# Wide modulation sets on VectorE, and products with a column of ones at their end

## The chip, the cores and the metric

The kernel runs on one core of a Trainium2 chip, as one program with one launch. The metric is the device time of an execution in microseconds (us), from the median of several runs. The engines are named as in the profile: PE is TensorE's products and PEld its weight loads, DVE is VectorE, ACT is ScalarE, POOL is GpSimd, SP is SyncE, whose queue issues the transfers.

## What is computed

One layer of an encoder block on 256 tokens of width 2048, in float32, with adaLN modulation from one conditioning vector `c`:

```python
c_act = jax.nn.silu(c)
mod = (c_act @ ada_w[l] + ada_b[l])[:, None, :]
shift_a, scale_a, gate_a, shift_f, scale_f, gate_f = jnp.split(mod, N_MOD, axis=-1)

h = rmsnorm(x, norm1_w[l]) * (1.0 + scale_a) + shift_a
proj = h @ w_in[l]
...
mixed = jnp.concatenate([ret_out, mla_out], axis=-1) @ w_o[l]
x = x + gate_a * mixed

h = rmsnorm(x, norm2_w[l]) * (1.0 + scale_f) + shift_f
ff = (jax.nn.silu(h @ w_gate[l]) * (h @ w_up[l])) @ w_down[l]
x = x + gate_f * ff
```

`ret_out` comes from eight retention heads with rotary positions and decay, `mla_out` from eight attention heads with compressed latents. `ada_w` is 2048 by 12288, so the one vector `c_act` meets 100 MB of weights, a third of all that the kernel reads. Each of the six sections (shift, scale and gate for the mixer, the same for the feed-forward) has 2048 columns.

## The kernel before, in words

All weights are streamed from memory in the order of use. A projection's weights come in tiles of 512 KB (tile `stg`, six buffers). `split_weights` (L119) issues the transfer on SP, lets ScalarE round the tile to a high part (`whi`, L124) and VectorE subtract it for a low part (`wlo`, L126), three buffers each. TensorE multiplies in three passes, high by high, high by low, low by high (L132 to L134), with 512 columns moving. `run` (L152) walks a list of steps; up to three tiles are loaded and split ahead of the step that uses them (`LOOK`).

The modulation is made by `ada_set` (L174). A set is `nk` times 128 columns of one section. Its weights come in the same 512 KB tiles, one **unit** each. A string of 0 and 1 says for each set which engine takes it:

- on TensorE (L196), the vector in a padded 32-column tile `c_pad` is the stationary operand and 256 columns move; the bank is copied to `ada_acc` by ScalarE at the end (L206);
- on VectorE, each row block of the unit is multiplied by the vector's value of its partition and added to the accumulator `ada_acc` (L198 the first time, L200 after), at the width of the set, 512 columns at most.

The 128 partitions of the accumulator have to be summed at a set's end. `finish` (L202) adds the bias row of a gate section (L211, L212). `spread` (L214) handles the two kinds of sections: for a gate it multiplies the accumulator by a matrix of ones (L218), which lays the sum on all partitions; for shift and scale it transposes each 128 columns (L222) so that VectorE can reduce them to a column (L226), then adds the bias (L227) and, for a scale section, makes the gain (L230).

The two sections that the input projection needs are made beside its column groups. The mixer's own list is `plan` (L742 to L786): the input projection's last chunks, latent and attention steps (`mla_step`), retention heads (`ret_scores`, `ret_out`) with tiles of the output projection as filler, and the rest of that projection. The sections GT_A (the mixer's gate) and SC_F, SH_F (scale and shift of the feed-forward, their first 1536 columns) are cut into ten sets, `early`; their 80 units are put between the plan's steps (L791 to L805) by two counters, one of TensorE time, one of transfer time, at a rate `ADA_RATE`. `ADA_PE2` gives sets 1, 6 and 7 of them to TensorE. VectorE's order in time is made by a scheduler from this list, so small VectorE work such as the rotary tables (L296 to L306, 32 operations on 128x96) can stand elsewhere than in the code.

## Time and profile before

| | us |
|---|---|
| median of three runs | 1261.68 |
| the three runs | 1259.57, 1261.85, 1261.68 |
| the profiled execution's own time | 1259.87 |
| its span, first to last instruction | 1257.9 |
| PE busy | 1217.3 (97%) |
| PEld busy | 973.0 (77%) |
| DVE busy | 841.1 (67%) |
| ACT busy | 600.9 (48%) |
| mean granted clock of TensorE | .994 |

The durations in this document come from that one profiled execution; its time is 1.8 us under the median. A busy time is the union of an engine's instructions, so overlapping instructions count once. An instruction's own duration is longer than its distance to the next one where the two overlap; for a price the distance from start to start is read. A float32 product of TensorE leaves two records and two weight loads in the trace, a transposition one of each.

### The profile page before, as it was taken

To read this page: it belongs to the slowest core of one execution; us is meant where nothing else is said; L and a number is where in the kernel's file an instruction comes from. 1 tells how busy PE (TensorE), PEld (TensorE's weight loads), DVE (VectorE), ACT (ScalarE), POOL (GpSimd) and SP (SyncE) were. 2 spreads that over 40 slices of the span, in tenths; PEclk is the share of its full clock that TensorE was granted. 3 is DMA by queue.
4 is the path that set the end of the run, shared out by engine and by line. 5 is a ranking of instruction groups with operands and counts; after the bars stand their busy time and mean duration, and the time that the engine had idled before them with its cause. 6 is when DMAs were issued, how large, how long until landed. Compare 5 with 4: busy or idle time off the path is not lost.

```text
span 1257.9 us, 16210 instructions
## 1 busy us (share of the span) xinstructions
PE 1217.3 (97%) x6022; PEld 973.0 (77%) x6022; DVE 841.1 (67%) x1157; ACT 600.9 (48%) x812; POOL 2.2 (0%) x10
## 2 busy tenths in 40 slices
PE   5899999999999999899999999999999999999997
PEld 2676667789886787678888888888888888888885
DVE  2596988889997997885555556656655454554544
ACT  4553454545557554745444444444444443444433
POOL 0000000000000000000000000000000000000000
PEclk9999999999999999899999999999999999999999
DMA  8989898888878987897676658766775655555562
GB/s 330 324 302 310 296 326 295 291 311 298 323 243 297 319 289 268 323 356 222 218 226 225 202 170 284 235 198 212 262 224 189 218 188 197 194 191 194 191 200 85
DMA packets 88800, 315.28 MB, mean 251 GB/s; under 512 B 10249, under 2 KB 10377, under 8 KB 88209
## 3 DMA queue, kind: packets, MB, share of 16 engines
q1 hardware_dynamic: 88720, 314.24, 73.4%
q8 instruction: 47, 0.77, 0.2%
q14 instruction: 33, 0.26, 0.1%
HBM read 312.11 MB, written 2.10 MB: 250 GB/s over the span
## 4 chain that ended last, share of the span: by engine, by line
PE 85%; DVE 7%; DMA 4%; ACT 2%; issue 2%; SPq 0%; ACTq 0%; DVEq 0%
PE bank L133 25%; PE bank L134 25%; PE bank L132 25%; DMA stg<-in_stream 4%; DVE wlo L126 3%; PE bank L196 3%; PE bank L148 2%; DVE ada_acc L200 2%; ACT whi L124 1%; PE bank L625 1%; PE bank L614 1%; PE bank L513 0%; PE bank L537 0%; PE bank L512 0%; PE bank L222 0%
## 5 line engine op out<-in xcount | busy, mean ns | idle before, releaser
L126 DVE TENSOR_TENSOR wlo<-stg,whi 128x1024 fp32r<-128x1024 f32 (+2 forms) x400 | 478.8, 1199 | 331.8 <-ACT whi L124 330.3
L124 ACT CAST whi<-stg 128x1024 fp32r<-128x1024 f32 (+2 forms) x400 | 413.2, 1034 | 526.1 <-PE bank L134 411.9
L132 PE MATMUL bank<-whi,actt 128*128 128x512 f32 (+1 forms) x1184 | 457.7, 392 | 11.4 <-ACT whi L124 8.2
L133 PE MATMUL bank<-wlo,actt 128*128 128x512 f32 (+1 forms) x1184 | 460.7, 389 | 6.9 <-DVE wlo L126 6.2
L134 PE MATMUL bank<-whi,actt 128*128 128x512 f32 (+1 forms) x1184 | 458.1, 387 | 0.2 <-DVE actt L145 0.2
L132 PEld LDWEIGHTS bank<-whi,actt 128*128 128x128 f32 x1184 | 221.8, 189 | 63.6 <-ACT whi L124 12.0
L133 PEld LDWEIGHTS bank<-wlo,actt 128*128 128x128 f32 x1184 | 223.2, 189 | 61.5 <-DVE wlo L126 16.7
L134 PEld LDWEIGHTS bank<-whi,actt 128*128 128x128 f32 x1184 | 223.1, 188 | 44.8 <-DVE actt L145 0.9
L200 DVE SCALAR_TENSOR_TENSOR ada_acc<-stg,c_act,ada_acc 128x512 f32<-128x512 f32 (+1 forms) x240 | 175.3, 731 | 21.2 <-DMA stg<-in_stream 18.3
L132 PE MATMUL bank<-whi,ap 128*128 128x512 f32 x352 | 137.0, 389 | 0.0
L134 PE MATMUL bank<-whi,ap 128*128 128x512 f32 x352 | 136.9, 389 | 0.0
L133 PE MATMUL bank<-wlo,ap 128*128 128x512 f32 x352 | 136.9, 389 | 0.0
L132 PEld LDWEIGHTS bank<-whi,ap 128*128 128x128 f32 x352 | 66.1, 188 | 13.8
L133 PEld LDWEIGHTS bank<-wlo,ap 128*128 128x128 f32 x352 | 66.1, 188 | 13.7
L134 PEld LDWEIGHTS bank<-whi,ap 128*128 128x128 f32 x352 | 66.1, 188 | 13.6
L196 PE MATMUL bank<-stg,c_pad 128*32 128x256 f32 x544 | 48.6, 418 | 11.4 <-DMA stg<-in_stream 11.3
L196 PEld LDWEIGHTS bank<-stg,c_pad 128*32 128x32 f32 x544 | 13.0, 112 | 35.5 <-issue 26.7
L851 ACT ACTIVATE sgs<-bank 128x512 f32<-128x512 f32 x22 | 13.1, 597 | 10.5 <-PE bank L134 9.8
L145 DVE TENSOR_TENSOR actt<-hfull,actt 128x256 fp32r<-128x256 f32 x40 | 16.3, 419 | 2.4 <-ACT actt L144 2.3
L853 DVE TENSOR_TENSOR sgs<-bank,sgs 128x512 f32<-128x512 f32 x22 | 14.3, 683 | 0.6 <-PE bank L134 0.6
L833 DVE TENSOR_TENSOR ap<-bank,ap 128x512 fp32r<-128x512 f32 x22 | 14.1, 682 | 0.0
L226 DVE TENSOR_REDUCE mod<-bank 128x4 f32<-128x512 f32 (+3 forms) x18 | 8.0, 444 | 8.9 <-PE bank L222 8.7
(219 smaller groups left out, 708.2 us busy)
## 6 DMA issues: line engine op xcount, KB each, us to landing
stg<-in_stream SPq DMA_DIRECT2D x568, 512.0 KB, 4.4
stg<-in_stream SPq DMA_DIRECT2D x16, 288.0 KB, 3.5
stg<-in_stream SPq DMA_DIRECT2D x8, 384.0 KB
xt<-in_x SPq DMA_DIRECT2D x2, 1024.0 KB
acc_cq<-in_x SPq DMA_DIRECT2D x8, 256.0 KB, 4.7
out<-x SPq DMA_DIRECT2D x8, 256.0 KB, 2.9
acc_k<-in_rows SPq DMA_DIRECT2D x1, 1024.0 KB, 7.5
fw<-in_rows SPq DMA_DIRECT2D x1, 1024.0 KB
```

What stands on the lines that cost most here:

```text
L124: S.copy(hi, stg)
L126: V.tensor_tensor(lo, stg, hi.bitcast(F32), op=ALU.subtract)
L132: PE.matmul(o, lhsT=ah, rhs=whi, start=first, stop=False)
L133: PE.matmul(o, lhsT=ah, rhs=wlo, start=False, stop=False)
L134: PE.matmul(o, lhsT=al, rhs=whi, start=False, stop=last)
L145: V.tensor_tensor(dst[:, k, T:2 * T], tmp, dst[:, k, 0:T].bitcast(F32), op=ALU.subtract)
L148: PE.transpose(b[:, j, tb * P:(tb + 1) * P], src, ident)
L196: PE.matmul(a[q:q + 32, c:c + wide], lhsT=c_pad[:, k], rhs=w[:, j], start=c == 0 and k < 4, stop=c + wide == n and k >= KT - 4)
L200: V.scalar_tensor_tensor(out=a, in0=w[:, j], scalar=c_act[:, k:k + 1], in1=a, op0=ALU.mult, op1=ALU.add)
L833: V.tensor_tensor(ap[:, ks, T:2 * T], b, ap[:, ks, 0:T].bitcast(F32), op=ALU.subtract)
L851: S.activation(sg, o[tb], AF.Silu)
L853: V.tensor_tensor(sg, o[tb], sg, op=ALU.mult)
```

## The change

Five things change in `ada_set` and around it.

1. Sets that VectorE makes may be 1024 columns wide. GT_A becomes two sets of eight blocks (before, four of four), SC_F and SH_F a set of eight and one of four each. A unit then holds one row block of 1024 columns and takes one operation in place of two.
2. The end of a shift or scale set is a product of each 128x128 block, as the stationary operand, with one column of ones. Its result is the wanted column, so the reduction is gone and one addition from the bank remains.
3. A gate set on VectorE begins with a clear by GpSimd and a transfer of the bias row into row 0 of the accumulator, and its first step accumulates too. The addition at the end is gone.
4. `ADA_PE2` leaves one set, the narrow one of SC_F, on TensorE; two sets' worth of units goes to VectorE.
5. The 80 units are spread evenly: after each step of the plan as many units as its share of the plan's cost (2.7 for a tile, 1 for any other step), so that they are through at 95% of it.

The angle tiles of the rotary tables take buffers of the decay tiles' tag, and the tile `dg` those of `hfull`.

```diff
--- before.py
+++ after.py
@@ -40,9 +40,8 @@
 GROUPS = [(0, 2), (2, 4), (6, 4), (10, 6)]
 ADA_PE = "10010100101101"
 LEAD = [1, 1, 3, 3, 3, 3, 3]
-ADA_PE2 = "010000110000"
-ADA_RATE = 0.8
-ADA_AHEAD = 0
+ADA_PE2 = "000100"
+ADA_END = 0.95
 LOOK = 3
 FILL_A = [2, 2]
 FILL_M = [3, 0, 1, 0, 4, 2, 1, 3, 2, 2]
@@ -178,7 +177,8 @@
         acc = {}
 
         def acc_tile():
-            return (pool or late["pool"]).tile([P, n], F32, name="ada_acc", tag="ada_acc", bufs=2 if pool else 1, padded_shape=[P, 512])
+            most = 1024 if pool else 512
+            return (pool or late["pool"]).tile([P, n], F32, name="ada_acc", tag="ada_acc", bufs=2 if pool else 1, padded_shape=[P, most])
 
         def load(c, t):
             w = wp.tile([P, kk, wide], F32, name="stg", tag="stg", bufs=6)
@@ -188,16 +188,23 @@
         def body(c, t, w):
             if c == 0 and t == 0:
                 acc["t"] = bank() if on_pe else acc_tile()
+                if not on_pe and rowdst is not None:
+                    G.memset(acc["t"], 0.0)
+                    bias_row(acc["t"])
             a = acc["t"]
             for j in range(kk):
                 k = t * kk + j
                 if on_pe:
                     q = 32 * (k % 4)
                     PE.matmul(a[q:q + 32, c:c + wide], lhsT=c_pad[:, k], rhs=w[:, j], start=c == 0 and k < 4, stop=c + wide == n and k >= KT - 4)
-                elif k == 0:
+                elif k == 0 and rowdst is None:
                     V.tensor_scalar(out=a, in0=w[:, j], scalar1=c_act[:, 0:1], scalar2=None, op0=ALU.mult)
                 else:
                     V.scalar_tensor_tensor(out=a, in0=w[:, j], scalar=c_act[:, k:k + 1], in1=a, op0=ALU.mult, op1=ALU.add)
+
+        def bias_row(a):
+            r0 = (R_GA if sec == GT_A else R_GF) + k0 * P
+            SY.dma_start(a[0:1, :], rows[:, r0:r0 + n])
 
         def finish():
             a = acc["t"]
@@ -205,26 +212,25 @@
                 b, a = a, acc_tile()
                 S.copy(a, b[:, 0:n])
             acc["a"] = a
-            if rowdst is not None:
-                r0 = (R_GA if sec == GT_A else R_GF) + k0 * P
+            if on_pe and rowdst is not None:
                 br = wp.tile([1, n], F32, name="bias_row", tag="stg", bufs=6)
-                SY.dma_start(br, rows[:, r0:r0 + n])
+                bias_row(br)
                 V.tensor_tensor(a[0:1, :], a[0:1, :], br, op=ALU.add)
 
         def spread():
             a = acc["a"]
+            if rowdst is not None:
+                for c in range(0, n, CH):
+                    b = bank()
+                    PE.matmul(b, lhsT=ones, rhs=a[:, c:c + CH], start=True, stop=True)
+                    S.copy(rowdst()[:, k0 * P + c:k0 * P + c + CH], b)
+                return
             b = bank()
-            if rowdst is not None:
-                PE.matmul(b[:, 0:n], lhsT=ones, rhs=a, start=True, stop=True)
-                S.copy(rowdst()[:, k0 * P:k0 * P + n], b[:, 0:n])
-                return
             for j in range(nk):
-                PE.transpose(b[:, j * P:(j + 1) * P], a[:, j * P:(j + 1) * P], ident)
+                PE.matmul(b[:, j:j + 1], lhsT=a[:, j * P:(j + 1) * P], rhs=ones[:, 0:1], start=True, stop=True)
             ks = slice(sec * KT + k0, sec * KT + k0 + nk)
             m = mod[:, ks]
-            parts = b[:, 0:n].rearrange("p (j q) -> p j q", q=P)
-            V.tensor_reduce(out=m, in_=parts[:, :, ::32] if on_pe else parts, axis=AX.X, op=ALU.add)
-            V.tensor_tensor(m, m, col[:, C_ADAB + ks.start:C_ADAB + ks.stop], op=ALU.add)
+            V.tensor_tensor(m, b[:, 0:nk], col[:, C_ADAB + ks.start:C_ADAB + ks.stop], op=ALU.add)
             if sec in (SC_A, SC_F):
                 g, nw = (gain_a, C_N1) if sec == SC_A else (gain_f, C_N2)
                 V.scalar_tensor_tensor(out=g[:, k0:k0 + nk], in0=m, scalar=1.0, in1=col[:, nw + k0:nw + k0 + nk], op0=ALU.add, op1=ALU.mult)
@@ -291,8 +297,8 @@
         SY.dma_start(freq, rows[:, R_FREQ:R_FREQ + 96].partition_broadcast(P))
         V.tensor_copy(posf, post)
         for tb in range(NB):
-            a = mid.tile([P, 96], F32, name="ang", tag="ang", bufs=2)
-            n = mid.tile([P, 96], F32, name="turns", tag="turns", bufs=2)
+            an = mid.tile([P, 2, 96], F32, name="ang", tag="dec", bufs=2)
+            a, n = an[:, 0], an[:, 1]
             V.tensor_scalar(out=a, in0=freq, scalar1=posf[:, tb:tb + 1], scalar2=None, op0=ALU.mult)
             for magic in (1.5 * 2.0 ** 34, 1.5 * 2.0 ** 23):
                 V.tensor_scalar(out=n, in0=a, scalar1=1.0 / TWO_PI, scalar2=magic, op0=ALU.mult, op1=ALU.add)
@@ -722,7 +728,7 @@
         rsqrt(stat[:, 30:32], stat[:, 28:30], 1.0 / D)
         b = bank()
         for tb in range(NB):
-            dg = mid.tile([P, P], F32, name="dg", tag="dg", bufs=2)
+            dg = mid.tile([P, P], F32, name="dg", tag="hfull", bufs=2)
             V.tensor_scalar(out=dg, in0=ident, scalar1=stat[:, 30 + tb:31 + tb], scalar2=None, op0=ALU.mult)
             PE.matmul(b[:, tb * P:(tb + 1) * P], lhsT=ones, rhs=dg, start=True, stop=True)
         S.copy(rstd_b, b[:, 0:T])
@@ -785,23 +791,19 @@
             plan.append(f(turn_x2, n - 1))
         plan += c[2:]
 
-    early = [(GT_A, 4 * i, 4, lambda: gate_a) for i in range(4)]
-    early += [(sec, k, min(4, K_LATE - k), None) for sec in (SC_F, SH_F) for k in range(0, K_LATE, 4)]
+    early = [(GT_A, 8 * i, 8, lambda: gate_a) for i in range(2)]
+    early += [(sec, k, min(8, K_LATE - k), None) for sec in (SC_F, SH_F) for k in range(0, K_LATE, 8)]
     units = ada_stream(mid, [(*st, on == "1") for st, on in zip(early, ADA_PE2)])
-    pe = dma = 0.0
-    for s in plan:
+    cost = [2.7 if s[0] == "w" else 1.0 for s in plan]
+    done, used = 0.0, 0
+    for s, c in zip(plan, cost):
         steps.append(s)
-        if s[0] == "w":
-            pe += 2.6
-            dma += 1.5
-        else:
-            pe += 1.0
-        for _ in range(2):
-            if units and dma < pe * ADA_RATE + ADA_AHEAD:
-                steps += units.pop(0)
-                pe += 0.5
-                dma += 1.5
-    for u in units:
+        done += c
+        want = min(len(units), int(len(units) * done / (ADA_END * sum(cost))))
+        for u in units[used:want]:
+            steps += u
+        used = want
+    for u in units[used:]:
         steps += u
 
     def gate_f_tile():
```

Where the order of the instructions moves, it does so as follows. First VectorE, where the last column group of the input projection begins. `dec` is a decay tile of the retention, `ang`, `turns` and `sc_t` belong to the rotary tables, `wlo` to the weight split. Before, in the middle of the second column group, a little earlier than this place:

```order
L609 TENSOR_SCALAR dec<-dist,lg 128x384
L302 TENSOR_SCALAR sc_t<-ang 128x96
L610 SCALAR_TENSOR_TENSOR dec<-dist,lg,dec 128x384
L350 TENSOR_TENSOR acc_k<-acc_k,bank 128x512 x2
L126 TENSOR_TENSOR wlo<-stg,whi 128x1024
L303 TENSOR_SCALAR ang<-ang 128x96
L609 TENSOR_SCALAR dec<-dist,lg 128x384
L304 TENSOR_SCALAR turns<-ang 128x96
L610 SCALAR_TENSOR_TENSOR dec<-dist,lg,dec 128x384
L305 TENSOR_TENSOR ang<-ang,turns 128x96
L306 TENSOR_SCALAR sc_t<-ang 128x96
L126 TENSOR_TENSOR wlo<-stg,whi 128x1024
```

Now, right before the first accumulate of the first gate set:

```order
L305 TENSOR_SCALAR ang<-ang 128x96 x2
L307 SCALAR_TENSOR_TENSOR ang<-ang 128x96 x6
L308 TENSOR_SCALAR sc_t<-ang 128x96 x2
L309 TENSOR_SCALAR ang<-ang 128x96 x2
L310 TENSOR_SCALAR ang<-ang 128x96 x2
L311 TENSOR_TENSOR ang<-ang 128x96 x2
L312 TENSOR_SCALAR sc_t<-ang 128x96 x2
L125 TENSOR_TENSOR wlo<-stg,whi 128x576
L203 SCALAR_TENSOR_TENSOR ada_acc<-stg,c_act,ada_acc 128x1024
L356 TENSOR_TENSOR acc_cq<-acc_cq,bank 128x512 x2
```

The rotary operations have left the projection's middle and stand in one block ahead of the first 1024-column accumulate; the decay tiles stand later, in the attention steps.

Second, TensorE at the start of the retention steps. Before:

```order
L614 MATMUL bank<-qT,kT 128x256 x2
L148 MATMUL bank<-ident,rout 128x128 x8
L196 MATMUL bank<-stg,c_pad 32x256 x8
L614 MATMUL bank<-qT,kT 128x256 x2
L625 MATMUL bank<-acc_v,rP 128x128 x4
L196 MATMUL bank<-stg,c_pad 32x256 x4
L222 MATMUL bank<-ident,ada_acc 128x128 x4
L148 MATMUL bank<-ident,att 128x128 x8
```

Now:

```order
L620 MATMUL bank<-qT,kT 128x256 x2
L199 MATMUL bank<-stg,c_pad 32x256 x4
L147 MATMUL bank<-ident,rout 128x128 x8
L620 MATMUL bank<-qT,kT 128x256 x2
L631 MATMUL bank<-acc_v,rP 128x128 x4
L199 MATMUL bank<-stg,c_pad 32x256 x4
L230 MATMUL bank<-ones,ada_acc 128x1 x8
L147 MATMUL bank<-ident,att 128x128 x8
```

Modulation products (L196, now L199) are eight instead of twelve in these rows, and the four transpositions with the identity are products with the column of ones (L230), in two passes each.

Third, VectorE in the second half of the output projection, up to the first update of `x`. Before:

```order
L126 TENSOR_TENSOR wlo<-stg,whi 128x1024 x2
L200 SCALAR_TENSOR_TENSOR ada_acc<-stg,c_act,ada_acc 128x512 x2
L126 TENSOR_TENSOR wlo<-stg,whi 128x1024
L200 SCALAR_TENSOR_TENSOR ada_acc<-stg,c_act,ada_acc 128x512 x3
L126 TENSOR_TENSOR wlo<-stg,whi 128x1024
L684 TENSOR_TENSOR x_0_3928<-x_0_3928,bank 128x512
L684 TENSOR_TENSOR x_1_3936<-x_1_3936,bank 128x512
L685 TENSOR_TENSOR x_0_3928<-x_0_3928,gate_a 128x512
```

Now:

```order
L125 TENSOR_TENSOR wlo<-stg,whi 128x1024
L203 SCALAR_TENSOR_TENSOR ada_acc<-stg,c_act,ada_acc 128x1024
L125 TENSOR_TENSOR wlo<-stg,whi 128x1024
L201 TENSOR_SCALAR ada_acc<-stg,c_act 128x512
L203 SCALAR_TENSOR_TENSOR ada_acc<-stg,c_act,ada_acc 128x512 x2
L125 TENSOR_TENSOR wlo<-stg,whi 128x1024
L203 SCALAR_TENSOR_TENSOR ada_acc<-stg,c_act,ada_acc 128x512 x2
L690 TENSOR_TENSOR x_0_3793<-x_0_3793,bank 128x512
L125 TENSOR_TENSOR wlo<-stg,whi 128x1024
L691 TENSOR_TENSOR x_0_3793<-x_0_3793,gate_a 128x512
```

Where the last narrow accumulates stood, there is now a 1024-column one, and a narrow set (SH_F's second) only begins here (L201), so that it goes on behind the first update of `x`.

## Rows read from the trace of the kernel before

**Rows 1.** Windows by stage, all engines: length, busy us (instructions), granted clock, DMA share, GB/s.
```profile
24.00:192.00 168.00, 157.52 (x858) 113.29 (x858) 130.02 (x219) 82.55 (x115) 0.00 (x0) 0.99 0.88 307
192.00:261.00 69.00, 67.59 (x415) 52.27 (x413) 54.27 (x97) 36.61 (x63) 0.00 (x0) 1.00 0.86 298
261.00:376.00 115.00, 114.10 (x632) 97.72 (x633) 107.75 (x176) 63.44 (x119) 0.00 (x0) 1.00 0.85 294
376.00:434.00 58.00, 58.00 (x389) 42.22 (x389) 49.12 (x114) 37.34 (x65) 0.00 (x0) 1.00 0.84 305
434.00:490.00 56.00, 56.00 (x269) 46.74 (x268) 52.73 (x76) 32.94 (x50) 0.00 (x0) 1.00 0.88 300
490.00:503.00 13.00, 13.00 (x87) 9.34 (x87) 7.83 (x12) 4.83 (x11) 0.00 (x0) 1.00 0.57 187
```

**Rows 2.** The same windows, line L196 (modulation products on TensorE) alone.
```profile
192.00:261.00 69.00, 7.62 (x80) 1.83 (x80) 1.00 0.86 298
...
376.00:434.00 58.00, 10.02 (x128) 2.62 (x128) 1.00 0.84 305
```

**Rows 3.** The same windows, line L200 (modulation accumulates on VectorE) alone.
```profile
192.00:261.00 69.00, 11.21 (x15) 1.00 0.86 298
...
376.00:434.00 58.00, 8.92 (x12) 1.00 0.84 305
434.00:490.00 56.00, 13.45 (x19) 1.00 0.88 300
```

**Rows 4.** Window from 288 to 320 us, all engines (columns as in rows 1).
```profile
288.00:320.00 32.00, 31.41 (x210) 28.26 (x209) 30.65 (x51) 18.87 (x34) 0.00 (x0) 1.00 0.92 321
```

**Rows 5.** Timeline of TensorE around one modulation unit: start us, us, operation.
```profile
100.85 0.39 PE L134 MATMUL bank<-whi,actt 128*128 128x512 f32 x1
101.17 0.64 PE L196 MATMUL bank<-stg,c_pad 128*32 128x256 f32 x8
101.74 0.50 PE L132 MATMUL bank<-whi,actt 128*128 128x512 f32 x1
```

**Rows 6.** Timeline of VectorE in attention.
```profile
320.94 0.68 DVE L515 TENSOR_REDUCE st<-bank 128x2 f32<-128x512 f32 x1
321.54 0.74 DVE L200 SCALAR_TENSOR_TENSOR ada_acc<-stg,c_act,ada_acc 128x512 f32<-128x512 f32 x1
322.20 0.16 DVE L516 TENSOR_SCALAR st<-st 128x2 f32<-128x2 f32 x1
```

**Rows 7.** VectorE groups by shape: busy us, mean ns, idle before; last three: 140 to 172 us.
```profile
L200 DVE SCALAR_TENSOR_TENSOR ada_acc<-stg,c_act,ada_acc 128x512 f32<-128x512 f32 x225 | 168.0, 748 | 21.0 <-DMA stg<-in_stream 18.3
...
L200 DVE SCALAR_TENSOR_TENSOR ada_acc<-stg,c_act,ada_acc 128x256 f32<-128x256 f32 x15 | 7.2, 482 | 0.2
...
L301 DVE SCALAR_TENSOR_TENSOR ang<-turns,ang 128x96 f32<-128x96 f32 x12 | 2.7, 252 | 0.0
...
L610 DVE SCALAR_TENSOR_TENSOR dec<-dist,lg,dec 128x384 f32<-128x384 f32 x2 | 1.2, 618 | 0.0
L609 DVE TENSOR_SCALAR dec<-dist,lg 128x384 f32<-128x384 f32 x2 | 0.8, 415 | 0.0
```

**Rows 8.** Timeline of TensorE in the retention steps.
```profile
427.38 0.60 PE L222 MATMUL bank<-ident,ada_acc 128*128 128x128 f32 x4
427.82 1.06 PE L625 MATMUL bank<-acc_v,rP 128*128 128x128 f32 x8
428.71 1.03 PE L614 MATMUL bank<-qT,kT 128*128 128x256 f32 x4
```

**Rows 9.** Weight loads of TensorE by line: count, busy us, mean ns.
```profile
L625 PEld LDWEIGHTS bank<-acc_v,rP 128*128 128x128 f32 x64 | 8.0, 191 | 1.8 <-issue 1.6
...
L222 PEld LDWEIGHTS bank<-ident,ada_acc 128*128 128x128 f32 x64 | 7.6, 142 | 5.4 <-ACT ada_acc L206 2.2 <-issue 1.6 <-ACT dec L611 0.4
```

**Rows 10.** GpSimd groups by line and shape.
```profile
L259 POOL MEMSET c_pad<- 128x512 f32 x1 | 0.5, 525 | 0.0
```

**Rows 11.** DMA issues of the page: tile, count, KB each, median us from issue to landing.
```profile
stg<-in_stream SPq DMA_DIRECT2D x568, 512.0 KB, 4.4
```

## The prediction

> **What bounds the kernel now.** I read four views, from coarse to fine. The windows by stage come first [rows 1]. I cut the span where the work changes: input projection with the first two modulation sections (24 to 192 us), its last column group (192 to 261), attention and the second retention half (261 to 376), the retention steps (376 to 434), the output projection (434 to 503), and feed-forward. The reader is to compare, in each row, TensorE's busy time with the length: 157.52 of 168, then 67.59 of 69, 114.10 of 115, and 58.00 of 58, 56.00 of 56, 13.00 of 13. TensorE is the bound from 192 us on, at a granted clock of .99 to 1.00; it has 10.5 us of idle time before 192, and nearly none behind. VectorE is second: 107.75 of 115 (.937) in one stretch, 52.73 of 56 (.942) in another. So an edit pays only where it takes work off TensorE, and it costs where it lifts VectorE to the length of the stretch.
>
> The windows by line come second: who does the modulation units (one unit is 512 KB of modulation weights), in which stretch [rows 2, 3]. On TensorE a unit leaves 8 records: 80 records are 10 units in 192 to 261, and 128 are 16 in 376 to 434. On VectorE a unit is two 512-column operations: 15 accumulates plus the set's first multiply there are 8 units, and 19 plus one in 434 to 490 are 10.
>
> Third come timelines for prices (next part). Fourth comes the highest VectorE share that I found over 32 us ahead of the feed-forward: 30.65 of 32, which is .958, with TensorE at 31.41 [rows 4].
>
> **The change, part by part: the prices.**
>
> - A unit on TensorE. Between two neighbouring products of the projection the step is .23 us; across a unit's 8 records it is .89 (100.85 to 101.74) [rows 5]. So a unit costs .66 us of TensorE.
> - A 512-column accumulate on VectorE: .66 us from its start to the next (321.54 to 322.20); a reduction .60 (320.94 to 321.54) [rows 6].
> - A 1024-column accumulate: no row has one. The forms of 256 and 512 columns take 482 and 748 ns, 266 for each 256 columns more [rows 7]. So 512 columns more add .53 to the .66: 1.19 us. The upper bound is two narrow ones, 1.32. I take 1.19: it is the straight continuation of two rows of the same operation. A unit on VectorE thus falls from 1.32 to 1.19.
> - A transposition of the end of a set: four take .44 (427.38 to 427.82), .11 each. What replaces it is a product of the 128x128 accumulator, as stationary operand, with one column. No row has one. The nearest is the retention's fp32 product, same stationary shape, 128 columns moving: four in .89 (427.82 to 428.71), .22 each [rows 8]. It issues two weight loads of 191 ns where the transposition issues one of 142 [rows 9], and those loads do not shrink with the moving columns. Below, a product could cost what a transposition does, .11; above, both loads one after another, .38. I take .22, +.11 against the transposition: the row with the same loads.
>
> The Trainium skill ("TensorE: Matmul & The Clock Gate", Back-to-back issue gap) gives matmuls of 1 to 64 columns an issue floor of about 25 ns. Two passes would make an estimated .05 per product, and the sum would be 11 us lower over 64 products. The rows speak against it, since the two loads are there whatever the columns.
>
> - Gate sets on VectorE: the accumulator is cleared by GpSimd and the bias row lands in it by DMA before the first accumulate, in place of an add behind the last one. A 128x512 clear takes 525 ns, so some 1.0 for 1024 columns, and a transfer lands in 4.4 us [rows 10, 11]: 5.4 in all. In the order, the tile is asked for while 22 VectorE rows stand ahead of the first accumulate, so I cost it at nothing; without that cover it is up to 5.4 us once. SP waits for the clear, and the weight loads behind it on that queue wait too, but three tiles are ahead. Lower bound: 0.
>
> **The same by stretch.** The order shows where things now stand. The rotary tables (32 small VectorE operations) leave 147 to 168 us and stand as one block just ahead of the first wide accumulate. Four more units reach the output projection, seven fewer the retention steps.
>
> - 24 to 192. TensorE gets 24 products more dear by .11: +2.6. VectorE loses the rotary block, two decay tiles and three reductions. The block's 32 operations of 128x96 last up to 252 ns [rows 7]; an accumulate overlaps the next one by .09 (748 long, .66 apart), so I put them .14 apart, 4.4 us in all. A decay tile's two operations, 415 and 618 ns, come by the same overlap to .85, two tiles to 1.7, three reductions to 1.8: together 7.9 of 130.02. TensorE's 10.5 us of idle time covers most of the 2.6. I take -.3, between -3 (the idle time shrinks with VectorE's load) and +3.
> - 192 to 261. TensorE loses 8 of its 10 units, 5.3 us, and pays .4 for four products: 62.7. VectorE: 54.27 - 10.6 (16 narrow operations) + 20.2 (17 wide) + 4.4 (rotary) = 68.3 of 69. Here VectorE becomes the longer engine. At a share of 1 the stretch shrinks by .7; at the best share seen, .958, it takes 71.3, +2.3. Middle: **+1.0**, bounds -4.9 (TensorE alone decides) and +2.3.
> - 261 to 376. Four transpositions leave (-.4). VectorE gains the two decay tiles (+1.7) and loses 27 x 1.32 - 28 x 1.19 = 2.3, a reduction and the bias adds, so it is eased a little, and I let half of TensorE's .9 idle go: -.8, bounds -1.3 and 0.
> - 376 to 434. TensorE: 58.0 - 8 units (5.3) + 12 products (1.3) = 54.0. VectorE: 49.1 - 12 narrow accumulates (7.9) - 1.4 for their first multiply and the reductions + 10 x 1.19 = 51.7, which at .958 also gives 54.0. **-4.0**, bounds -4.3 and -2.5.
> - 434 to 503. TensorE: 12 products for 8 transpositions, +1.8. VectorE in 434 to 490: 52.7 - 12.5 (19 narrow) - 1.7 + 7 x 1.19 + 8 x 1.32 = 57.4 of 56, at .958 59.9, +3.9. The 13 us behind have VectorE at 7.83, but TensorE full, so lost time is not recovered. Middle: **+2.5**, bounds 1.8 and 3.9.
> - Feed-forward: 8 products (+.9) against two reductions: +.1, bounds -.5 and +.9.
>
> Sum: -.3 + 1.0 - .8 - 4.0 + 2.5 + .1 = **-1.5 us**. It is made against the profiled execution's 1259.87, which lies 1.8 below the median of the three runs; I set it against the median, 1261.68: **1260.2**. A measurement of this kernel can tell about .2%, 2.5 us, from no change.
>
> **The rivals.**
>
> *B, TensorE stays the bound.* VectorE runs at a share near 1 where it must, or work slides into neighbouring slack; then 192 to 261 shrinks by 4.9 and the output projection pays 1.8: -.3 - 4.9 - .8 - 4.0 + 1.8 + .1 = -8.1, 1253.6. For it: in 434 to 490 TensorE was at 56.00 of 56 with VectorE at .942, so that share costs nothing yet. Against it: 68.3 of 69 leaves no room for any wait.
>
> *C, slower: VectorE sets the pace where its share would pass what it has held.* The weight split of each tile queues behind wide accumulates that wait for their transfer, and TensorE waits for the split. Price: the share VectorE held over 115 us, .937, holds as a ceiling. Then 192 to 261 takes 68.3 / .937 = 72.9 (+3.9), 376 to 434 takes 55.2 (-2.8), 434 to 490 takes 61.3 (+5.3): -.3 + 3.9 - .8 - 2.8 + 5.3 + .1 = +5.4, 1267.1. It decides from a needed share of .94 on. Against it: .958 occurs without loss over 32 us.
>
> *D, slower by the gate bias.* The first wide accumulate waits the 5.4 us out, and the splits stand behind it: -1.5 + 5.4 = +3.9, 1265.6. The 22 rows ahead speak against it.
>
> *E, slower by the new ends.* The two loads of a one-column product run one after another, since so short a product hides nothing: .38 in place of .22, 64 x .16 = 10.2 more, 1270.4. The .22 spacing at two 191 ns loads speaks against it, but there a 128-column product ran meanwhile.
>
> A rule of the Trainium skill stands on E's side: "TensorE: Matmul & The Clock Gate", Terms, calls the transpose mode 4 times faster for FP32, so the change gives up a cheap form; by it a product would cost an estimated .44, 64 x .22 = 14.1 us over my price and 1274.3. The two rows of .11 and .22 show a factor of two for the same shapes, not four.
>
> That the change doesn't do what it says I rule out by the order: 64 transpositions became 64 products, and one modulation set of the mixer stays on TensorE.
>
> **How the numbers follow.** The forecast's chance is .50, of which .34 within .2% (it lies 1.0 us inside that bound) and .16 faster. B gets .22, faster. C gets .18, D .04, E .06, all slower. So faster .38, same .34, slower .28. The range reaches from just under B to C, 1253.0 to 1267.0; outside are the lower part of B (.07), the upper part of C (.05) and E (.06).
>
> **What would show it.** 128 fewer TensorE records of modulation products; wide accumulates some 1.27 long and 1.19 apart; one-column pairs .22 apart. VectorE's share at .95 or more in the last column group and the output projection, with weight loads there waiting for the split's low part. The retention steps are shorter by about 4. It is wrong if the last column group is shorter by 4 or more (B), if the output projection is longer by over 4 (C), if VectorE stands idle over 2 us ahead of the first wide accumulate of a gate (D), or if one-column products stand over .3 apart (E).

## The result, and the profile after

The changed kernel takes 1273.99 us (median of four runs, 1273.2 to 1275.23) against 1261.32 of the kernel before: a ratio of 1.011, 95% interval 1.0095 to 1.0125. It is slower by 12.7 us between the medians and by 12 to 16 by the interval, where 1.5 less was forecast, and lies above the range. The profiled execution has a span of 1272.2 us against 1257.9.

The windows of the changed kernel, all engines, cut at the same projection products of TensorE as [rows 1] (columns as there; PE and DVE busy are the first and third figures):

```profile
25.90:200.40 174.50, 163.04 (x882) 117.94 (x882) 121.43 (x176) 76.89 (x107) 0.00 (x0) 0.99 0.85 293
200.40:277.10 76.70, 68.93 (x360) 54.47 (x358) 65.15 (x127) 40.66 (x68) 1.91 (x2) 0.96 0.80 281
277.10:389.40 112.30, 111.95 (x625) 96.40 (x623) 103.30 (x143) 64.63 (x121) 0.00 (x0) 1.00 0.84 294
389.40:442.90 53.50, 53.50 (x336) 42.86 (x336) 47.49 (x105) 36.35 (x63) 0.00 (x0) 1.00 0.80 284
442.90:505.20 62.30, 60.04 (x285) 49.59 (x285) 58.77 (x77) 33.23 (x50) 0.00 (x0) 0.97 0.87 299
505.20:518.40 13.20, 13.20 (x89) 9.65 (x87) 7.29 (x13) 4.95 (x12) 0.00 (x0) 1.00 0.65 236
...
590.00:1272.00 682.00, 672.81 (x3008) 556.76 (x3006) 371.24 (x365) 286.68 (x311) 1.05 (x2) 1.00 0.61 205
```

The feed-forward is the same 682 us. The retention steps (389 to 443) really are shorter, 53.5 us for 58; the first part (174.5 for 168), the last column group (200 to 277, 76.7 for 69) and the output projection (443 to 505, 62.3 for 56) are longer. The delay builds up and falls back, read at the start of the same low-part subtraction on VectorE in both traces (400 of them, counted from 0):

| subtraction | 0 | 36 | 48 | 54 | 66 | 72 | 102 | 114 | 138 | 399 |
|---|---|---|---|---|---|---|---|---|---|---|
| before, us | 21.9 | 139.7 | 184.4 | 203.7 | 238.0 | 254.7 | 367.8 | 432.2 | 515.6 | 1241.6 |
| after, later by | 2.5 | 4.6 | 8.0 | 9.6 | 15.6 | 17.4 | 11.0 | 4.2 | 15.4 | 14.1 |

So 8 us are lost up to 184 us, 2.5 of them ahead of the first subtraction, and 9 in the last column group; 13 are won in attention and retention and 11 lost again in the output projection. These are VectorE's times. It splits tiles ahead of TensorE, and not always equally far: at the end of the retention steps it stands 4.2 us late, and TensorE, at its own product, 8.9. What a stretch costs is therefore read at TensorE's products below.

**The prices first.** The timeline of TensorE around the end of one set, after and then before:

```profile
136.49 0.95 PE L230 MATMUL bank<-ones,ada_acc 128*128 128x1 f32 x8
137.30 0.48 PE L131 MATMUL bank<-whi,actt 128*128 128x512 f32 x1
137.62 0.40 PE L132 MATMUL bank<-wlo,actt 128*128 128x512 f32 x1
```

```profile
132.35 0.60 PE L222 MATMUL bank<-ident,ada_acc 128*128 128x128 f32 x4
132.70 0.48 PE L132 MATMUL bank<-whi,actt 128*128 128x512 f32 x1
133.02 0.40 PE L133 MATMUL bank<-wlo,actt 128*128 128x512 f32 x1
```

From the first record of the end to the projection's second product it is 1.13 us with four products and .67 with four transpositions: .46 more, .115 each, and less the one .227 step in it .226 for a product against .11. The forecast had .22 and .11.

The wide accumulates of the changed kernel, as a group by shape and on the timeline of VectorE:

```profile
L203 DVE SCALAR_TENSOR_TENSOR ada_acc<-stg,c_act,ada_acc 128x1024 f32<-128x1024 f32 x62 | 79.3, 1279 | 5.1 <-DMA stg<-in_stream 5.0
```

```profile
226.08 1.28 DVE L203 SCALAR_TENSOR_TENSOR ada_acc<-stg,c_act,ada_acc 128x1024 f32<-128x1024 f32 x1
227.28 1.28 DVE L356 TENSOR_TENSOR acc_cq<-acc_cq,bank 128x512 f32<-128x512 f32 x2
```

1279 ns long and 1.20 us to the next instruction, where 1.27 and 1.19 were forecast from [rows 6, 7]. The prices hold. The sum that they were put into did not.

**The last column group.** The timeline of VectorE in the changed kernel, ahead of the first wide accumulate:

```profile
219.95 1.22 DVE L125 TENSOR_TENSOR wlo<-stg,whi 128x1024 fp32r<-128x1024 f32 x1
221.09 0.32 DVE L304 TENSOR_SCALAR ang<-ang 128x96 f32<-128x96 f32 x2
...
225.17 0.33 DVE L312 TENSOR_SCALAR sc_t<-ang 128x96 f32<-128x96 f32 x2
225.41 0.75 DVE L125 TENSOR_TENSOR wlo<-stg,whi 128x576 fp32r<-128x576 f32 x1
226.08 1.28 DVE L203 SCALAR_TENSOR_TENSOR ada_acc<-stg,c_act,ada_acc 128x1024 f32<-128x1024 f32 x1
```

Between one weight split and the next VectorE spends 4.3 us on the rotary tables alone. In that time it hands on no buffer of a split tile. The timeline of SyncE shows no weight tile issued between 221.20 and 226.19, and its waits from 213 to 231 us show 4.2 us for VectorE's subtraction:

```profile
221.20 0.33 SPq L185 DMA_DIRECT2D stg<-in_stream  x1
221.58 0.28 SPq L207 DMA_DIRECT2D ada_acc<-in_rows  x1
226.19 0.33 SPq L121 DMA_DIRECT2D stg<-in_stream  x1
```

```profile
SPq L121 <- DVE wlo L125: 8.7, 3, 4.2
```

The waits from 213 to 272 us in the changed kernel (engine, line and what it waited for, us in total, times, longest), and windows of the 24 us behind the block, whole and in part:

```profile
ACT whi L123 <- DMA stg<-in_stream: 7.6, 4, 4.3
PEld bank L131 <- ACT whi L123: 5.3, 4, 2.7
...
PEld bank L132 <- DVE wlo L125: 4.4, 7, 1.3
PE bank L131 <- ACT whi L123: 4.2, 3, 2.5
...
ACT sq L410 <- DVE acc_ck L356: 2.6, 1, 2.6
```

```profile
230.00:254.00 24.00, 18.73 (x92) 14.78 (x91) 20.60 (x39) 11.05 (x20) 0.00 (x0) 0.86 0.92 314
230.00:243.20 13.20, 8.85 (x55) 7.19 (x53) 11.23 (x17) 5.46 (x10) 0.00 (x0) 1.00 0.93 313
243.20:250.00 6.80, 5.88 (x13) 4.20 (x14) 6.80 (x17) 2.84 (x5) 0.00 (x0) 0.50 0.93 342
```

ScalarE waits for transfers, TensorE for ScalarE and VectorE. The longest wait of TensorE, 2.5 us up to 243.6, is for a rounding that ScalarE runs right behind two sums of squares (`sq`), and these had waited 2.6 us for VectorE's addition to `acc_ck`. TensorE is busy for 8.85 of the 13.2 us up to 243.2; then its granted clock is .50, the lower of its two levels, for 6.8 us, and neighbouring products of 512 columns start .43 us apart in place of .23. Its clock falls to the lower level in two more places where the kernel before had 1.00, each behind waits of TensorE:

```profile
161.00:165.00 4.00, 4.00 (x15) 3.14 (x12) 0.93 (x2) 1.77 (x2) 0.00 (x0) 0.57 0.98 353
458.30:461.70 3.40, 3.40 (x10) 2.64 (x9) 3.19 (x3) 0.69 (x2) 0.00 (x0) 0.51 0.84 235
```

Some 27 steps of .43 in place of .23 make an estimated 5.4 us of the 14 that are lost. At the same splits as 230 to 254 here, the kernel before had a clock of 1.00 and TensorE busy for 17.59 of 19 us:

```profile
219.00:238.00 19.00, 17.59 (x124) 14.15 (x122) 15.10 (x38) 9.43 (x19) 0.00 (x0) 1.00 0.90 299
```

**The output projection.** VectorE's accumulates by shape from 442.9 to 505.2 us in the changed kernel:

```profile
L203 DVE SCALAR_TENSOR_TENSOR ada_acc<-stg,c_act,ada_acc 128x512 f32<-128x512 f32 x15 | 11.2, 750 | 0.2
L203 DVE SCALAR_TENSOR_TENSOR ada_acc<-stg,c_act,ada_acc 128x1024 f32<-128x1024 f32 x8 | 10.2, 1276 | 0.0
L201 DVE TENSOR_SCALAR ada_acc<-stg,c_act 128x512 f32<-128x512 f32 x1 | 0.5, 478 | 0.0
```

Of the eight wide units one straddles the start; with the 16 narrow operations there are 15 units where [rows 3] had 10 (19 accumulates and a first multiply). VectorE is busy for 58.77 of 62.3 us, .943, and TensorE for 60.04, so it stands idle for 2.3.

### The profile page after: what moved, and what is told of

Read it like the earlier page. It is cut to its first block, busy times and chain, and to the rows that moved or that the text cites. A ratio compares the mean times of both kernels' runs of the same rounds, so it can differ in the third digit from the quotient of the medians.

```text
span 1272.2 us, 16032 instructions
## 1 busy us (share of the span) xinstructions
PE 1222.3 (96%) x5958; PEld 984.5 (77%) x5958; DVE 840.2 (66%) x1097; ACT 599.3 (47%) x809; POOL 5.7 (0%) x15
## 4 chain that ended last, share of the span: by engine, by line
PE 81%; DVE 10%; DMA 4%; issue 2%; ACT 2%; SPq 0%; ACTq 0%; DVEq 0%
PE bank L132 25%; PE bank L133 24%; PE bank L131 24%; DMA stg<-in_stream 4%; DVE wlo L125 3%; DVE ada_acc L203 3%; PE bank L199 2%; PE bank L147 2%; ACT whi L123 1%; PE bank L230 1%; PE bank L225 0%; PE bank L620 0%; PE bank L543 0%; PE bank L631 0%; PE bank L519 0%
## 5 line engine op out<-in xcount | busy, mean ns | idle before, releaser
L132 PE MATMUL bank<-wlo,actt 128*128 128x512 f32 (+1 forms) x1184 | 463.5, 392 | 10.3 <-DVE wlo L125 10.1
L203 DVE SCALAR_TENSOR_TENSOR ada_acc<-stg,c_act,ada_acc 128x512 f32<-128x512 f32 (+2 forms) x215 | 189.8, 883 | 21.8 <-DMA stg<-in_stream 18.6
L131 PEld LDWEIGHTS bank<-whi,ap 128*128 128x128 f32 x352 | 66.1, 188 | 13.8
L133 PEld LDWEIGHTS bank<-whi,ap 128*128 128x128 f32 x352 | 66.1, 188 | 13.8
L132 PEld LDWEIGHTS bank<-wlo,ap 128*128 128x128 f32 x352 | 66.1, 188 | 13.5
L199 PE MATMUL bank<-stg,c_pad 128*32 128x256 f32 x416 | 38.9, 428 | 12.8 <-DMA stg<-in_stream 12.6
L199 PEld LDWEIGHTS bank<-stg,c_pad 128*32 128x32 f32 x416 | 10.4, 113 | 32.8 <-issue 22.8
L230 PEld LDWEIGHTS bank<-ones,ada_acc 128*128 128x128 f32 x128 | 17.0, 200 | 5.6 <-ACT ada_acc L213 2.2
L853 ACT ACTIVATE sgs<-bank 128x512 f32<-128x512 f32 x22 | 13.1, 598 | 10.5 <-PE bank L133 9.8
L230 PE MATMUL bank<-ones,ada_acc 128*128 128x1 f32 x128 | 16.7, 252 | 1.1 <-DVE ada_acc L203 0.7
```

The source lines that it names most:

```text
L131: PE.matmul(o, lhsT=ah, rhs=whi, start=first, stop=False)
L132: PE.matmul(o, lhsT=ah, rhs=wlo, start=False, stop=False)
L133: PE.matmul(o, lhsT=al, rhs=whi, start=False, stop=last)
L199: PE.matmul(a[q:q + 32, c:c + wide], lhsT=c_pad[:, k], rhs=w[:, j], start=c == 0 and k < 4, stop=c + wide == n and k >= KT - 4)
L203: V.scalar_tensor_tensor(out=a, in0=w[:, j], scalar=c_act[:, k:k + 1], in1=a, op0=ALU.mult, op1=ALU.add)
L230: PE.matmul(b[:, j:j + 1], lhsT=a[:, j * P:(j + 1) * P], rhs=ones[:, 0:1], start=True, stop=True)
```

## The experiments

Fourteen kernels ran, four to twelve executions of each, each beside the kernel before on its chip, whose median there was 1258.6 to 1259.3. I compare the ratios across the batches; a ratio of 1.001 is 1.26 us.

| kernel | ratio to before | 95% interval | us over before |
|---|---|---|---|
| the change | 1.011 | 1.0095 to 1.0125 | 13.8 |
| a_transp | 1.0015 | 1.0001 to 1.0029 | 1.9 |
| a_rot | 1.0107 | 1.0088 to 1.0126 | 13.5 |
| a_oldpace | 1.011 | 1.0091 to 1.013 | 13.8 |
| b_prod | 1.0182 | 1.0163 to 1.02 | 22.9 |
| b_prod_pin | 1.007 | 1.0046 to 1.0094 | 8.8 |
| a_prod_pin | 1.0088 | 1.0064 to 1.0111 | 11.1 |
| a_transp_pin | 1.0069 | 1.0044 to 1.0095 | 8.7 |
| t_end85 | 1.0088 | 1.0064 to 1.0113 | 11.1 |
| t_tail | .997 | .9956 to .9984 | -3.8 |
| t_narrow | 1.0046 | 1.0029 to 1.0063 | 5.8 |
| t_pe3 | 1.0023 | 1.0007 to 1.0038 | 2.9 |
| t_oldpace | .9999 | .9987 to 1.0012 | -.1 |
| a_rotmix | 1.0082 | 1.0065 to 1.01 | 10.3 |
| t_oldtail | 1.0009 | .9997 to 1.002 | 1.1 |

The last column is the ratio less one, times 1259.

### First: which part of the change

**a_transp**, the change with the old ends:

```diff
...
-                PE.matmul(b[:, j:j + 1], lhsT=a[:, j * P:(j + 1) * P], rhs=ones[:, 0:1], start=True, stop=True)
...
-            V.tensor_tensor(m, b[:, 0:nk], col[:, C_ADAB + ks.start:C_ADAB + ks.stop], op=ALU.add)
+            for j0 in range(0, nk, 4):
...
+                    PE.transpose(b[:, j * P:(j + 1) * P], a[:, (j0 + j) * P:(j0 + j + 1) * P], ident)
+                V.tensor_reduce(out=m[:, j0:j0 + nj], in_=parts[:, :, ::32] if on_pe else parts, axis=AX.X, op=ALU.add)
+            V.tensor_tensor(m, m, col[:, C_ADAB + ks.start:C_ADAB + ks.stop], op=ALU.add)
```

> The changed kernel with the old end of a shift or scale set: transpositions and reductions in place of the products with a column of ones. Its order has the rotary tables back in the middle of the projection. Theory O (the products' side effect on the order: the rotary block ahead of the first wide accumulate costs some 9 us in the last column group): both go, 1274.0 - 9 - 5 = about 1260. Theory P (only the products' own time, 64 x .11 = 7 us): 1267. Theory U (the loss is made by the modulation units that now lie in the output projection, +10 us there): 1272 to 1274.

Measured 1259.87 us, 1.9 over before: with the products gone, 12 of the 14 us are gone. That is the 1260 of theory O, but by luck: O has 9 us for the place of the rotary block, and a_rotmix, below, finds 3.5.

**b_prod**, the kernel before with those products alone (the same lines the other way round, for sets of four):

> The kernel before with the products with a column of ones alone. Its order also has the rotary tables as one late block. Theory O: more than the products' own time: 1261.3 + 7 + up to 9 = 1268 to 1277, with the delay in the last column group. Theory P: 1261.3 + 7 = 1268, spread over the sets' ends. Theory U: within 2 us of 1261 apart from the products, so at most 1268.

Measured 1282.31, 22.9 over before. That is above what any of the three theories had. One edit, made in two kernels, costs 12 us in the one and 23 in the other: up to three times 7.4 us, the products' own time (64 of .115). In the order of this kernel too the rotary tables are one late block (217 to 222 us). Its sets are narrow, and in the last column group VectorE is busy for only 61.9 of 79.9 us; TensorE still loses 10.9 us there.

**a_rot** moves that block away whole:

```diff
-        if gi == 2:
+        if gi == 1:
             steps.append(f(rotary_tables))
```

> The changed kernel, products kept, with the rotary tables listed one column group earlier, so that their block stands far ahead of the first wide accumulate. Theory O: 1274.0 - 9 = about 1265, with the stretch from the first to the last weight split of the last column group shorter by 9. Theory P: no change, 1274. Theory U: no change, 1274.

Measured 1272.34, ratio 1.0107: nothing gained. In the trace the last column group gives 5 us back (subtractions 54 to 66 take 35.3 us in place of 40.2), and the group where the block now stands takes 60.2 for subtractions 18 to 36 in place of 55.7. My theory of the block's place fell here; that its being one block costs time stayed possible.

**a_oldpace**, the change with the old counters and rate in place of the even spread (the hunk of the diff at `cost`, reversed):

> The changed kernel with the old pace of the units (two counters and a rate). Theory U: the output projection gives back its 10 us and the retention steps take back some of their 13, so 1264 to 1274 by where the units land; the part that the even pace itself costs is read from the two stretches. Theories O and P: within 2 us of 1274, since the rotary block stays where it is and the products stay.

Measured 1273.9: no difference. Theory U falls: at the end of the output projection this kernel is 16.2 us late where the change is 15.4 late, with other units in it.

### Second: the products' time apart from the order

The order of the instructions is made by a scheduler from the program. So that an operation could be exchanged without a new order, I held the instructions of TensorE, VectorE, ScalarE and SyncE to a given order (GpSimd's stay free): the list `ORDER` was made from another kernel's built program, and each instruction gets an order-only dependence on the one before it on its engine.

```diff
     run(steps)
+    pin_order(tc)
...
+        for a, b in zip(q, q[1:]):
+            tc.add_manual_dep(b, a.name, mybir.DependencyInfo(mybir.DependencyClass.NoSync, mybir.DependencyReason.DATA), reason="pin")
```

**b_prod_pin**: products, in the order of the kernel before.

> The kernel before with the products with a column of ones, and with the order of every instruction on TensorE, VectorE, ScalarE and SyncE held to that of the kernel before (products where the transpositions stood, reductions gone). Theory Q (a product costs its own .12 us more of TensorE than a transposition, 64 x .116 = 7.4, and the rest of the 23 us of the products alone is the order that the scheduler makes with them): 1258.9 + 7.4 = 1266. Theory R (the products themselves hold up the engines, by their loads and the later end of a set, whatever the order): 1282, as without the hold. A part of the 7.4 can lie in idle time ahead of 192 us: down to 1263.

Measured 1268.01, 8.8 over before, against 22.9 with the order that the scheduler makes with the products. The products' own price is 8.8 (5.8 to 11.8) and the order's is 14. In the traces TensorE's and ScalarE's operations stand in the order of the kernel before, one for one. No kernel was held to its own order, so what the hold itself costs, if anything, is not measured and would be part of the 8.8.

**a_prod_pin**: the change, in the order of a_transp. **a_transp_pin**: the opposite.

> The changed kernel, products kept, with the order of every instruction on the four engines held to that of the changed kernel with transpositions. Theory Q: 1259.9 + 64 x .116 = 1267, at least 1263. Theory R: 1274, as the changed kernel.

> The opposite: transpositions and reductions in the changed kernel, with the order held to that of the changed kernel (the rotary tables late, in a block). Theory Q: 1274 - 7.4 + what 18 reductions cost VectorE where it is nearly full (0 to 5) = 1267 to 1272, so worse than the same work in its own order, 1259.9. Theory R: 1260.

Measured 1269.5 (11.1 over before) and 1267.84 (8.7 over). With the change itself and a_transp the four make a square:

| us over before | order of a_transp | order of the change |
|---|---|---|
| transpositions | 1.9 | 8.7 |
| products | 11.1 | 13.8 |

The products cost 9 in the one order and 5 in the other; the order costs 7 with transpositions and 3 with products. Each of these has an uncertainty of some 3 us, so the last, 3, is not clear of nothing. Theory Q is borne out by b_prod_pin (1266 expected, 1282 by R) and by a_transp_pin (1267 to 1272, R 1260); for a_prod_pin, 1269.5 lies between Q's 1267 and R's 1274, nearer to Q. The order alone slows the same work.

**a_rotmix**: the change in its own order, but with the 32 rotary operations scattered as in a_transp.

> The changed kernel with its own order of all instructions, except that the rotary tables' 32 operations stand where the kernel with transpositions has them, scattered among 147 to 168 us. If the block ahead of the first wide accumulate is what the order costs in the last column group (there 5 us went when the block was moved away whole, and 5 came back at the new place), 1274.0 - 5 = 1269; if scattered operations cost as much as a block, 1274.

Measured 1269.8, 3.5 less than the change, and the trace has the gain in the right place: the same subtractions come 1.1 us earlier at number 54, 3.8 at 66, 4.0 at 72, and 3.8 at the end. The lower level of TensorE's clock comes here too, but for 6.8 us in all where the change has 13.7. The timeline of VectorE in this kernel, at the place where the block stood:

```profile
225.19 1.37 DVE L357 TENSOR_TENSOR acc_cq<-acc_cq,bank 128x512 f32<-128x512 f32 x2 [2.10 <-PE bank L134]
226.47 0.75 DVE L126 TENSOR_TENSOR wlo<-stg,whi 128x576 fp32r<-128x576 f32 x1
227.14 1.28 DVE L204 SCALAR_TENSOR_TENSOR ada_acc<-stg,c_act,ada_acc 128x1024 f32<-128x1024 f32 x1
```

VectorE now waits 2.1 us for TensorE instead of the reverse. So the block costs some 3.5 us where it stands whole. In pieces it shows no loss at its new place: subtractions 36 to 48 take 46.5 us, and 48.1 in the change.

### Third: what the other parts give, on transpositions

The kernels from here on have the old ends, as a_transp has, and the diffs show what differs from it. None is held to an order, so each measures its edit and the new order together.

**t_narrow**: ten narrow sets, one on TensorE.

```diff
-ADA_PE2 = "000100"
+ADA_PE2 = "0000001000"
...
-    early = [(GT_A, 8 * i, 8, lambda: gate_a) for i in range(2)]
-    early += [(sec, k, min(8, K_LATE - k), None) for sec in (SC_F, SH_F) for k in range(0, K_LATE, 8)]
+    early = [(GT_A, 4 * i, 4, lambda: gate_a) for i in range(4)]
+    early += [(sec, k, min(4, K_LATE - k), None) for sec in (SC_F, SH_F) for k in range(0, K_LATE, 4)]
```

> The changed kernel with transpositions and with the ten narrow sets of before, one of them on TensorE: 56 units that were 1024 columns wide take two operations. By the rows VectorE gets 56 x .13 = 7.3 us more, and two more gate sets' ends. If VectorE sets the pace in the stretches where it is nearly full, 1260 + 4 to 7; if TensorE and the transfers set it, 1260.

5.8 over before, 4 over a_transp (some 1 to 7), in the range expected if VectorE's time counts. How much of the 4 is the width's and how much the new order's is not shown.

**t_pe3**: the three sets of before on TensorE, the others wide.

```diff
-ADA_PE2 = "000100"
+ADA_PE2 = "0100110"
...
+    early = [(GT_A, k, n, lambda: gate_a) for k, n in ((0, 4), (4, 4), (8, 8))]
+    early += [(SC_F, 0, 8, None), (SC_F, 8, 4, None), (SH_F, 0, 4, None), (SH_F, 4, 8, None)]
```

> The changed kernel with transpositions, wide sets and even pace, but with the same three sets on TensorE as before (4 blocks of the gate, 4 of SC_F, 4 of SH_F). TensorE gets 16 units x .66 = 10.6 us more, VectorE 16 x 1.19 = 19 less. If TensorE's time decides, 1260 + 10.6 = 1270; if moving the sets to VectorE gave nothing because VectorE sets the pace there, 1256 to 1260.

2.9 over before, 1 over a_transp, where TensorE's 10.6 us were at stake; neither of the two answers expected. Moving two sets to VectorE gave nothing that the time shows.

**t_oldpace** (transpositions, wide sets, old pace):

> The changed kernel with transpositions and the old pace. If the even pace pays for what the output projection loses with what the retention steps gain, 1260; if the even pace itself costs, 1255; if it is what keeps the wide sets from hurting, 1265.

Measured .1 under before, 2 under a_transp, near the edge of what can be told. The even pace gives nothing that the time shows.

**t_end85** (transpositions, `ADA_END = 0.85`):

> Transpositions, wide sets and even pace, but the 80 units through at 85% of the plan in place of 95%. If the 4.5 us wait of TensorE for VectorE at the end of the output projection (482 to 486 us) comes from units that lie too late, it goes, and the time is 1259.9 - 4 = 1256 or less; if the units only fill VectorE earlier, 1260.

11.1 over before, a clear miss. The wait did go, to .5 us, but at subtraction 114 this kernel stands 3.4 us behind the kernel before, where a_transp is 12 ahead. One number moved, the scheduler made another order, and 9 us went, nearly all ahead of the output projection; which operations cost them is not shown.

**t_tail.** The expectation of t_end85 named a real wait, but its remedy brought a whole new order with it. The timeline of TensorE in a_transp at the end of the output projection:

```profile
481.85 0.39 PE L133 MATMUL bank<-whi,actt 128*128 128x512 f32 x1
486.55 0.99 PE L234 MATMUL bank<-ident,ada_acc 128*128 128x128 f32 x4 [4.31 <-DVE ada_acc L203]
```

and VectorE's, with the accumulate that it waits for:

```profile
485.66 0.74 DVE L203 SCALAR_TENSOR_TENSOR ada_acc<-stg,c_act,ada_acc 128x512 f32<-128x512 f32 x1
```

The last set's end follows its last unit without a gap, so its transpositions stand on TensorE ahead of work that is ready. The remedy is one line; the end then stands behind the mixer's plan:

```diff
-        want = min(len(units), int(len(units) * done / (ADA_END * sum(cost))))
+        want = min(len(units) - 1, int(len(units) * done / (ADA_END * sum(cost))))
```

> Wide sets, even pace, transpositions at the sets' ends, and the end of the last set held back until the mixer's plan is through. In the order, only that end moves. If the 4.3 us in which TensorE waited at 482 us for the last set's accumulates was time on the path, 1259.9 - 4.3 = 1255.6, some 3 us under the kernel before (ratio .9975). If the time only moves behind, to the modulation products that follow, 1260.

Measured 1255.39 (twelve runs), ratio .997, .9956 to .9984: 3.8 us under the kernel before and the best of all. The order is a_transp's but for that end. The profiled execution is the slowest of the twelve, 1260.48, and is read for the end alone. The trace has it at its new place, beside the modulation products that come next, with no wait ahead of it:

```profile
501.33 0.60 PE L234 MATMUL bank<-ident,ada_acc 128*128 128x128 f32 x4
501.86 1.93 PE L199 MATMUL bank<-stg,c_pad 128*32 128x256 f32 x32
```

**t_oldtail**, the same hold with the old pace:

> Wide sets, transpositions, the old pace, and the end of the last set held back as in the best kernel so far. If the old pace also leaves a wait at that end, under 1256; if the wait came from the even pace alone, as the old pace without the hold, 1258.

1.1 over before, no gain over t_oldpace. The wait belonged to the even pace: in t_oldpace TensorE waits .33 us at that end, in a_transp 4.31.

## Why the prediction was wrong

**The prices were right, point by point.** A product .226 us for .22, a wide accumulate 1.20 for 1.19, the rotary block 4.3 for 4.4. The gate bias cost little: the first wide accumulate starts as soon as VectorE is through with the split ahead of it, at 226.08, so rival D did not come.

**The step that failed is the sum by stretch**, in which I set each engine's load beside the other's and took the longer, at a share between .958 and 1, as if the order in which the work stands cost nothing. The table has what each stretch took more than in the kernel before, read at the same projection product of TensorE in both traces:

| stretch of the kernel before, us | forecast | the change | a_transp | a_prod_pin | a_transp_pin |
|---|---|---|---|---|---|
| up to 192 | -.3 | 8.4 | 1.0 | 5.1 | 6.1 |
| 192 to 261 | +1.0 | 7.6 | -.3 | 1.8 | 5.7 |
| 261 to 376 | -.8 | -2.6 | -3.5 | -1.9 | -2.1 |
| 376 to 434 | -4.0 | -4.5 | -4.9 | -4.5 | -4.9 |
| 434 to 503 | +2.5 | 6.4 | 8.6 | 12.8 | 4.5 |
| behind | +.1 | -1.2 | -1.2 | -1.2 | -1.1 |

Each column is one execution. The trace of t_tail, with a_transp's order up to its end, has 3.6 in 192 to 261 where a_transp has -.3, so a cell can be off by some 4 us. Three terms are short by 4 us or more: up to 192, 192 to 261 and 434 to 503. The other three came within 2 us, all on the fast side.

In the last column group I had 68.3 us of VectorE work in 69 us and forecast +1.0, at most +2.3. The stretch took 76.7, with VectorE busy for 65.15, a share of .849. In 288 to 320 us of the same kernel VectorE is at .987 and TensorE loses nothing:

```profile
288.00:320.00 32.00, 32.00 (x205) 29.04 (x204) 31.58 (x51) 20.70 (x42) 0.00 (x0) 1.00 0.92 326
```

So .958 was no ceiling, and a share under it no promise. What the runs show in its place is the order. In this stretch the order of the change costs some 6 us more than that of a_transp, with transpositions (5.7 against -.3) and with products (7.6 against 1.8). I had the block of 4.4 us in the order and priced it as load. As a block it kept SyncE's next weight tile waiting 4.2 us, and it cost some 3.5 us of time (a_rotmix). The 4.7 us that this stretch still loses with the block in pieces (a_rotmix) are not traced to single operations.

Of the 8.4 us up to 192, 1.9 are there at 24 us already, 2.7 are the products, an estimated 1.6 the lower clock and 1.0 more idle time of TensorE; the rest stays open.

**The term for the products was mis-sized in place, not in price.** I let most of 24 of them, 2.6 us, go into TensorE's idle time ahead of 192 us. In b_prod_pin that idle time is 11.0 us with the products and was 10.5 without, so none of them went into it. With the order held they cost 8.8 us in the kernel before (5.8 to 11.8) and 9 and 5 in the changed one: all of the 7.4 us that the rows give, as far as can be told.

**The units were counted rightly in the terms.** The sentence ahead of the stretches, four units more in the output projection and seven fewer in the retention steps, does not agree with them: they have five more (15 for 10) and four to five fewer. The trace has 15 in the projection, seven wide and eight narrow as priced, and 17 in the retention steps where the kernel before had 22.5. The retention steps came as forecast, -4.5 for -4.0. The projection's 6.4 for 2.5 is no matter of the count: the products' 1.8, TensorE's idle time of 2.3 (none before) and an estimated 1.6 for the lower clock make 5.7 of it.

**What the change gave without its products** (a_transp): my terms less those for products come to about -6; measured +1.9 (.1 to 3.7). The wait at the last set's end held 4 to 6 us of it (t_tail). Of the rest, the wide sets gave 4 against narrow ones (t_narrow), the assignment and the pace nothing that shows.

**The rivals.** E came nearest in time, 1270.4 and 1274.3, by luck, for its reason is refuted by the trace: products stand .112 apart by record, not two loads one after another. The Trainium skill's rule that the transpose mode is 4 times faster for FP32 ("TensorE: Matmul & The Clock Gate", Terms) is not what these shapes show: .226 to .11 is a factor of two. The Trainium skill's issue floor of about 25 ns for few columns ("TensorE: Matmul & The Clock Gate", Back-to-back issue gap) would have made a product an estimated .05; the one column did not make it cheaper than 128 did, .226 to .22. C had the right sign, but not the mechanism: the last column group lost at a VectorE share of .849, b_prod lost more there at .78, and at .943 in the output projection TensorE was idle for 2.3 us only. No rival had the order that the scheduler makes as a cost of its own, though the order shown ahead of the prediction had the block in it.

## What to carry to other kernels

Where a scheduler makes the order, an edit has two prices, its own and that of the new order, and the second can be the larger: hold the order to the old one and measure both. Compare stretches of two traces at the same work of the engine that bounds them, not at that of one which runs ahead. A stretch with two nearly full engines is not forecast by their totals; look for the longest run of one engine's work between two handovers, and for ends of work that stand in a queue ahead of what is ready. Idle time in a stretch does not by itself hide added work: 24 products left TensorE's as long as it was.

## What was not expected of the hardware

A float32 product with one moving column costs .226 us, the same as one with 128 (.22), at weight loads of 200 and 191 ns ([rows 9] has the second):

```profile
L230 PEld LDWEIGHTS bank<-ones,ada_acc 128*128 128x128 f32 x128 | 17.0, 200 | 5.6 <-ACT ada_acc L213 2.2 <-issue 1.2 <-PE bank L133 1.0
```

And TensorE's clock: a stretch in which TensorE waits can cost a second time. From 30 us to the end of the output projection the granted clock was at the lower of its two levels (1.2 for 2.4 GHz) for 13.7 us in the change, for 10.2 in b_prod, and never in the kernel before and in b_prod_pin, which has b_prod's operations in the order of the kernel before.
